# Down product of a hybrid decoder block: block results added to the residual in memory by one adding transfer

## The chip, the cores and the metric

The kernel runs on one core of one Trainium2 chip, in one launch. The metric is device time in microseconds. The engines are named as the profile names them: PE is TensorE (matmul), PEld its weight loads, DVE is VectorE, ACT is ScalarE, POOL is GpSimd, SP is SyncE, which here only issues transfers. The time before is 2142.49 us, the median of three runs (2139.59 to 2144.26).

## The reference

One decoder block on 512 rows of width 2048, in float32: a normalised input goes through a projection into two token mixers, their concatenated outputs through an output projection onto the residual, and then comes the channel mixer, which is where the change lies:

```python
x = x + jnp.einsum('bse,ed->bsd', y, w_out[l])
h = _rmsnorm(x, norm2_g[l])
up = jnp.einsum('bsd,df->bsf', h, ffn_w_up[l])          # 2048 -> 12288
up = _causal_dwconv(up, ffn_conv_w[l], ffn_conv_b[l])
gate, val = jnp.split(up, 2, axis=-1)
x = x + jnp.einsum('bsf,fd->bsd', jax.nn.gelu(gate) * val, ffn_w_down[l])  # 6144 -> 2048
return _rmsnorm(x, final_g)
```

## The kernel before, in words

**Matmul form.** A float32 operand is split into a rounded part h (ACT copy, L115) and the rest l (DVE subtraction, L116), and a product is three matmuls, h·h, h·l and l·h. The up and down products also use a fast scheme of seven block products for a 2 by 2 block product (the Strassen–Winograd form). A *unit* is one weight tile of four 128 by 256 pieces: it is loaded (512 KB, SP queue), VectorE forms three sums of its pieces (`sums`, L585 to L587; for activations L610 to L612), and the seven resulting operands are split (`pair`, L115 and L116). A unit is then 7 products of 6 matmuls (L753), 42 in all, issued in the order `ORDER = (1, 2, 6, 5, 3, 7, 4)`.

**PSUM.** Each of the seven products accumulates in a bank of its own over all units of a block; there are eight banks in rotation, so the next block's first product has a free bank, and each later one needs a bank that has been read out by ScalarE or VectorE.

**Stages.** The up product runs 24 blocks of 8 units; the seven results of a block are combined by `combine` (one ACT copy, seven VectorE operations) into two padded tiles, on which the width-3 convolution, the gelu and the gating work in later steps. The gated rows are stored to memory as `ad`. The down product has K = 6144 cut into three chunks of 8, 8 and 6 units and a tail of 512, and the output into four columns n of 512. It runs 12 blocks (chunk, column), each `size` units long. The residual of each column lives in memory as `x2d[n]`, 512 x 512 float32, 1 MB, laid out as 128 partitions of 8 KB. The tail does the last 512 of K with plain matmuls, one output row group at a time, together with the final norm.

**A down block.** In its second unit (in the seventh for the first block) GpSimd issues the load of `x2d[n]` into `xs[n]`, one of two 8 KB-per-partition tiles (L854, L855). At the block's end four ACT copies and three VectorE additions read the seven banks (L863 to L869): each of the three additions adds one bank to one quarter of `xs[n]`. Eight more VectorE operations (L871 to L878) are postponed by `later` to the next block's first four units, two after each. After the last two, GpSimd stores `xs[n]` back to `x2d[n]` (L891). The last chunk's columns 2 and 3 are not stored but stay in SBUF for the tail; columns 0 and 1 are loaded again for it (L900).

**Order.** In this part each engine executes its instructions in the order in which the code emits them. `prepare(ready(u))` is emitted before unit u's matmuls and keeps three steps going along one stream of weight and activation items: loads two items ahead, sums one ahead, splits up to the item before unit u+3's. The stream's tiles are triple-buffered (raw, h and l). Around each change of chunk the eight activation items of the next chunk are interleaved with the weight items, so there VectorE and ScalarE have up to two items a unit. GpSimd's queue in the down product holds only the residual loads and stores, and at the end four loads of the final gain (L905).

Of the kernel before, what the change touches and what calls it, by code (L numbers as in the profile page):

```python
# [8 lines left out]
F32 = mybir.dt.float32  # L9
# [3 lines left out]
ALU = mybir.AluOpType  # L13

P = 128
# [3 lines left out]
NS = S // P  # L19
# [48 lines left out]
def hybrid_block(ctx: ExitStack, tc: tile.TileContext, x, xT, w_in, w_out, w_up, w_dn, w_dl, wab, wsT, vec, bs, vgb, fg, out):  # L68
    nc = tc.nc
    const = ctx.enter_context(tc.tile_pool(name="const", bufs=1))  # L70
    def pool(name, side, bufs=1):
        return tc.alloc_tile_pool(name=name, bufs=bufs, side=side, reuse_waits="tile")
# [395 lines left out]
    for i in range(2):  # L468
        for st in range(NS):
            t = vv[i][:, st]  # L470
# [5 lines left out]
    for i in range(2):  # L476
        ps = project(w_in, B_U + i, xg, True)
# [161 lines left out]
    stream = []  # L639
# [117 lines left out]
    def later(step, f):  # L757
        lazy.setdefault(step, []).append(f)

    def t_tile(name, shape, bufs=1):  # L760
        return pools["t"].tile(shape, F32, name=name, tag=name, bufs=bufs)
# [1 line left out]
    def flat(q):  # L763
        return q.rearrange("p t n -> p (t n)")

    def combine(q, c1, c11, c12, c21, c22):

        tt = nc.vector.tensor_tensor
        nc.scalar.copy(c1, q[1])
        tt(c11, c1, q[2], ALU.add)  # L770
        v, w = t_tile("v", [P, 2, 256]), t_tile("w", [P, 2, 256])
        tt(v, q[6], c1, ALU.subtract)
        tt(w, q[5], v, ALU.add)
        tt(c12, w, q[3], ALU.add)
        tt(c22, w, q[7], ALU.add)
        tt(v, v, q[7], ALU.add)
        tt(c21, q[4], v, ALU.subtract)

    gates = {}

    def up_block(g, val, u0):
        q = {}
        for m in range(8):
            prepare(ready(u0 + m))
            for p in ORDER:
                product(q, p, act[m], stream[place[u0 + m]].hl, True, m == 0, m == 7)
            if m == 7 and u0 == 0:
                pads[:] = [t_tile(f"pad{n}", [P, 2, S + 2]) for n in range(2)]
                for t in pads:
                    nc.gpsimd.memset(t[:, :, 0:2], 0.0)  # L790
            for f in lazy.pop(u0 + m, ()):
                f()
        c1 = t_tile("c1", [P, 2, 256])
        lo, hi = slice(2, 258), slice(258, 514)
        combine(q, c1, pads[0][:, :, lo], pads[1][:, :, lo], pads[0][:, :, hi], pads[1][:, :, hi])
        if u0 == 0:
            pools["ps"].release()
            pools["tr"].release()
            pools["ps"] = psum("q1", 8)

        def tap(n, j, f):
            if val:
                dst = t_tile("cv", [P, 2, S])if j == 0 else cvs[n]
                cvs[n] = dst
            else:
                if j == 0:
                    gates[n] = t_tile("gate", [P, 2, S], 2)
                dst = gates[n]
            nc.scalar.activation(dst[:, j], pads[n][:, j, 2:2 + S], AF.Identity, bias=col(V_FB + f), scale=col(V_FW + 2 * 96 + f))

        def rest(n, j, f):
            dst = (cvs if val else gates)[n][:, j]
            for i in (1, 0):
                nc.vector.scalar_tensor_tensor(dst, pads[n][:, j, i:i + S], col(V_FW + i * 96 + f), dst, ALU.mult, ALU.add)
            if val:
                gate = gates[n][:, j]
                nc.vector.tensor_tensor(gate, gate, dst, ALU.mult)
                at = 0 if j else 2
                nc.gpsimd.dma_start(ad[2 * g + n][:, at:at + 2], gate.rearrange("p (a b) -> p a b", a=2))  # L819

        def gelu(n, j):
            t = gates[n][:, j]
            nc.scalar.activation(t, t, AF.Gelu_apprx_tanh)

        cvs = {}
        at = u0 + 8
        for i, (n, j) in enumerate(((1, 0), (1, 1), (0, 0), (0, 1))):
            f = 48 * val + 4 * g + 2 * n + j
            step = at + (0, 1, 3, 4)[i]
            later(step, lambda n=n, j=j, f=f: tap(n, j, f))  # L830
            later(step + 1, lambda n=n, j=j, f=f: rest(n, j, f))
            if not val:
                later(step + 2, lambda n=n, j=j: gelu(n, j))
# [9 lines left out]
    def down_block(ci, n, u0):  # L843
        tt = nc.vector.tensor_tensor
        size = len(CHUNKS[ci])
        q = {}
        for m in range(size):
            prepare(ready(u0 + m))
            if m == (6 if u0 == n_up else 1):
                if u0 == n_up:  # L850

                    pools["t"].release()
                    pools["x"] = pool("tx", "right")
                xs[n] = pools["x"].tile([P, NS, 512], F32, name="xs", tag="xs", bufs=2)  # L854
                nc.gpsimd.dma_start(xs[n], x2d[n])  # L855
            for p in ORDER:
                product(q, p, act[m], stream[place[u0 + m]].hl, False, m == 0, m == size - 1)
            for f in lazy.pop(u0 + m, ()):
                f()
        X = xs[n]  # L860
        X11, X12, X21, X22 = X[:, 0:2, 0:256], X[:, 0:2, 256:512], X[:, 2:4, 0:256], X[:, 2:4, 256:512]
        c1, c6, c5, c7 = (pools["x"].tile([P, 2, 256], F32, name="cc", tag="cc", bufs=4) for _ in range(4))
        nc.scalar.copy(c1, q[1])  # L863
        tt(X11, X11, q[2], ALU.add)
        nc.scalar.copy(c6, q[6])
        nc.scalar.copy(c5, q[5])
        tt(X12, X12, q[3], ALU.add)
        nc.scalar.copy(c7, q[7])
        tt(X21, X21, q[4], ALU.add)  # L869
        steps = [  # L870
            lambda: tt(X11, X11, c1, ALU.add),  # L871
            lambda: tt(c6, c6, c1, ALU.subtract),
            lambda: tt(c5, c5, c6, ALU.add),
            lambda: tt(X12, X12, c5, ALU.add),
            lambda: tt(c6, c6, c7, ALU.add),
            lambda: tt(X21, X21, c6, ALU.subtract),
            lambda: tt(c5, c5, c7, ALU.add),
            lambda: tt(X22, X22, c5, ALU.add),  # L878
        ]
        if u0 + size == len(units):  # L880
            prepare(len(stream) - 2)
            for f in steps:
                f()
            prepare(len(stream) - 1)
            return
        at = u0 + size
        for i in range(4):
            later(at + i, steps[2 * i])
            later(at + i, steps[2 * i + 1])
        if ci < 2 or n < 2:  # L890
            later(at + 3, lambda: nc.gpsimd.dma_start(x2d[n], X))  # L891

    for ci, s in enumerate(starts):
        for n in range(4):
# [12 lines left out]
    for st in range(NS):  # L907
# [4 lines left out]
        for n, (i, d, lo, hi) in enumerate(pieces):  # L912
# [5 lines left out]
                mm3(ps, a, w, f == 0, f == 3)  # L918
            t = xs[d][:, st, lo:hi]
            nc.vector.tensor_tensor(t, t, ps, ALU.add)  # L920
            sq = pools["x"].tile([P, 512], F32, name="sq", tag="cc", bufs=4)
            nc.scalar.activation(sq[:, 0:hi - lo], t, AF.Square, accum_out=ss3[:, st, n:n + 1])
            if last_rows and n < 3:
                nc.gpsimd.tensor_tensor(t, t, fgb[d][:, lo:hi], ALU.mult)
# [13 lines left out]
        for n in order:  # L938
# [7 lines left out]
                nc.scalar.mul(t, t, r)  # L946
            eng = nc.scalar if last_rows and n % 2 == 0 else nc.sync
            eng.dma_start(out[st * P:(st + 1) * P, d * 512 + lo:d * 512 + hi], t)
    for p in (pools["x"], pools["ps"], pools["a2"], pools["a1"], wq):
        p.release()  # L950


# [51 lines left out]
```

## Time and profile before

| | |
|---|---|
| median of three runs | 2142.49 us (2139.59 to 2144.26) |
| the profiled execution | 2140.87 us |
| its span, first to last instruction | 2139.2 us |
| mean granted TensorE clock | 0.982 |
| PE busy | 2065.3 us (97%) |
| DVE busy | 1806.6 us (84%) |
| ACT busy | 905.5 us (42%) |
| POOL busy | 59.6 us (3%) |
| loads `xs<-x2d` | 12 of 1 MB, median 5.7 us from issue to landing |
| stores `x2d<-xs` | 10 of 1 MB, median 4.7 us in the down product |

The page gives busy time by engine, then the span in 40 slices of 53.5 us with a digit for the busy tenths of each. The up product takes roughly slices 12 to 30, the down product 31 to 39, the tail is the last one. Matmul records overlap, so a busy PE is not PE at its peak, and a few matmul records can be missing. A row of the timeline or of the chain of waits begins with its start in us from the span's start and its duration; a bracket behind a row gives the idle time of the engine before it and what ended it. A row of a group gives count, busy time, mean and idle time before.

### The profile page before, as it was taken

Reading aid. Unit: us, or ns where it says so; the run is one execution under the profiler, and the core shown is the slowest. Engines: PE = TensorE matmul, PEld = TensorE weight load, DVE = VectorE, ACT = ScalarE, POOL = GpSimd, SP = SyncE. Lnnn points to the kernel's source line nnn. Section 1 sums busy time; section 2 is a strip of 40 time slices with the busy share of each in tenths; the row PEclk is TensorE's granted clock in tenths of the full one; section 3 lists DMA queues with packets and bytes.
Section 4 is the critical chain, followed back from the end, with each engine's and each line's share of the span. In section 5 each row is a group of like instructions: output and inputs, shape, how many; then the busy total and the mean of one; then the engine's idle time right before and its main releaser. Section 6 shows DMA issues by size and latency. Waiting matters only on the chain.

```text
span 2139.2 us, 34631 instructions
## 1 busy us (share of the span) xinstructions
PE 2065.3 (97%) x14552; PEld 1944.5 (91%) x14552; DVE 1806.6 (84%) x2341; ACT 905.5 (42%) x891; POOL 59.6 (3%) x118
## 2 busy tenths in 40 slices
PE   9999999999789999999999999999988998999998
PEld 7888888888679999999999999999978997998996
DVE  7588972744369999999999999999999999989986
ACT  5445322413244444444444444444444344444443
POOL 0000000100000000000000000000000000000001
PEclk9999999999889999999999999999989999999999
DMA  6222322533013333333333333333335454544563
GB/s 233 87 93 85 112 88 96 172 134 138 40 50 119 116 114 121 117 118 119 119 119 119 119 119 119 119 117 121 119 119 174 149 172 166 179 148 166 197 214 121
DMA packets 68605, 275.14 MB, mean 129 GB/s; under 512 B 8160, under 2 KB 8800, under 8 KB 58720
## 3 DMA queue, kind: packets, MB, share of 16 engines
q1 hardware_dynamic: 57888, 224.01, 32.4%
q0 software_dynamic: 9984, 48.24, 6.1%
q8 instruction: 114, 1.87, 0.4%
q10 hardware_dynamic: 576, 0.66, 0.1%
q14 instruction: 43, 0.35, 0.0%
HBM read 241.43 MB, written 31.46 MB: 128 GB/s over the span
## 4 chain that ended last, share of the span: by engine, by line
PE 47%; issue 39%; DVE 10%; DMA 2%; ACT 1%; POOL 1%; SPq 0%; POOLq 0%; DVEq 0%; ACTq 0%
PE qs L753 18%; PE ps L153 8%; PE ps L151 8%; PE ps L152 8%; DVE wl L116 3%; DVE al L116 2%; POOL ad L819 1%; PE tr L673 1%; DVE q L585 1%; DMA q<-w_dn 1%; PE qs L152 1%; PE qs L153 1%; PE qs L151 1%; DVE q L610 1%; DMA q<-ad 1%
## 5 line engine op out<-in xcount | busy, mean ns | idle before, releaser
L753 PE MATMUL qs<-ah,wh 128*128 128x256 f32 x2688 | 765.1, 285 | 4.9 <-ACT ah L115 2.4
L753 PE MATMUL qs<-ah,wl 128*128 128x256 f32 x2688 | 764.1, 284 | 5.7 <-DVE wl L116 5.7
L753 PE MATMUL qs<-al,wh 128*128 128x256 f32 x2688 | 764.1, 284 | 1.5 <-DVE al L116 1.5
L115 ACT CAST wh<-q 128x1792 fp32r<-128x1792 f32 (+1 forms) x282 | 476.8, 1691 | 669.5 <-PE qs L753 437.4
L116 DVE TENSOR_TENSOR wl<-q,wh 128x1792 fp32r<-128x1792 f32 (+1 forms) x282 | 567.7, 2013 | 24.9 <-ACT wh L115 24.8
L753 PEld LDWEIGHTS qs<-ah,wl 128*128 128x128 f32 x2688 | 519.5, 193 | 6.1 <-DVE wl L116 6.1
L753 PEld LDWEIGHTS qs<-ah,wh 128*128 128x128 f32 x2688 | 519.6, 193 | 5.8 <-ACT ah L115 2.6
L753 PEld LDWEIGHTS qs<-al,wh 128*128 128x128 f32 x2688 | 519.6, 193 | 1.8 <-DVE al L116 1.8
L753 PE MATMUL qs<-wl,ah 128*128 128x256 f32 x1232 | 355.1, 288 | 16.4 <-DVE wl L116 16.4
L753 PE MATMUL qs<-wh,ah 128*128 128x256 f32 x1232 | 354.3, 288 | 9.6 <-ACT cc L863 4.1
L753 PE MATMUL qs<-wh,al 128*128 128x256 f32 x1232 | 353.8, 287 | 4.8 <-DVE al L116 4.8
L753 PEld LDWEIGHTS qs<-wl,ah 128*128 128x128 f32 x1232 | 241.5, 196 | 18.8 <-DVE wl L116 18.7
L753 PEld LDWEIGHTS qs<-wh,ah 128*128 128x128 f32 x1232 | 241.8, 196 | 11.2 <-ACT cc L863 4.5
L753 PEld LDWEIGHTS qs<-wh,al 128*128 128x128 f32 x1232 | 241.6, 196 | 5.2 <-DVE al L116 5.2
L116 DVE TENSOR_TENSOR wl<-wraw,wh 128x1024 fp32r<-128x1024 f32 (+2 forms) x105 | 118.1, 1126 | 147.6 <-ACT wh L115 147.3
L115 ACT CAST wh<-wraw 128x1024 fp32r<-128x1024 f32 (+2 forms) x105 | 102.2, 974 | 275.6 <-PE ps L152 145.3
L585 DVE TENSOR_TENSOR q<-q 128x512 f32<-128x512 f32 x280 | 191.9, 685 | 15.5 <-DMA q<-w_dn 9.2
L151 PE MATMUL ps<-xgh,wh 128*128 128x512 f32 x384 | 152.4, 397 | 1.7 <-ACT wh L115 1.7
L152 PE MATMUL ps<-xgl,wh 128*128 128x512 f32 x384 | 152.1, 397 | 0.0
L153 PE MATMUL ps<-xgh,wl 128*128 128x512 f32 x384 | 150.5, 397 | 0.0
L586 DVE TENSOR_TENSOR q<-q 128x256 f32<-128x256 f32 x280 | 119.0, 425 | 9.7
L587 DVE TENSOR_TENSOR q<-q 128x256 f32<-128x256 f32 x280 | 119.0, 425 | 9.6
(241 smaller groups left out, 2303.9 us busy)
## 6 DMA issues: line engine op xcount, KB each, us to landing
q<-w_up SPq DMA_DIRECT2D x192, 512.0 KB, 3.5
q<-w_dn SPq DMA_DIRECT2D x88, 512.0 KB, 3.5
wraw<-w_in SPq DMA_DIRECT2D x28, 1024.0 KB, 4.9
wraw<-w_out SPq DMA_DIRECT2D x16, 1024.0 KB, 4.9
ad<-gate POOLq DMA_DIRECT2D x48, 256.0 KB, 2.3
q<-ad SPq DMA_DIRECT2D x24, 512.0 KB, 3.2
xs<-x2d POOLq DMA_DIRECT2D x12, 1024.0 KB, 5.7
x2d<-xs POOLq DMA_DIRECT2D x10, 1024.0 KB, 4.7
```

The lines of the kernel that those rows point to most:

```text
L115: nc.scalar.copy(h, src)
L116: nc.vector.tensor_tensor(l, src, h.bitcast(F32), ALU.subtract)
L151: nc.tensor.matmul(ps, lhsT=ah, rhs=bh, start=start, stop=False)
L152: nc.tensor.matmul(ps, lhsT=ah, rhs=bl, start=False, stop=False)
L153: nc.tensor.matmul(ps, lhsT=al, rhs=bh, start=False, stop=stop)
L585: nc.vector.tensor_tensor(q[:, 2:4], q[:, 5:7], q[:, 7:8].broadcast_to([P, 2, 256]), ALU.add)
L586: nc.vector.tensor_tensor(q[:, 1], q[:, 2], q[:, 6], ALU.add)
L587: nc.vector.tensor_tensor(q[:, 0], q[:, 1], q[:, 4], ALU.add)
L610: nc.vector.tensor_tensor(q[:, 2:4], q[:, 7:8].broadcast_to([P, 2, 256]), q[:, 5:7], ALU.subtract)
L673: nc.tensor.matmul(ps[:, st * P:(st + 1) * P], lhsT=x2[k // 4][:, st, (k % 4) * P:(k % 4 + 1) * P], rhs=diag[st], start=True, stop=True)
L753: nc.tensor.matmul(q[p][:, t], lhsT=x_, rhs=y_, start=first and t == 0 and n == 0, stop=last and t == 1 and n == 2, skip_group_check=True)
L819: nc.gpsimd.dma_start(ad[2 * g + n][:, at:at + 2], gate.rearrange("p (a b) -> p a b", a=2))
```

## The change

In the down product, the block's result is no longer added to the residual by VectorE. `combine`, the routine of the up product, writes the four quarters of the result into a tile `c` of its own (two buffers of the size that the `xs` tiles had), and GpSimd issues one transfer from `c` to `x2d[n]` with `accum_op=ALU.add`, which adds the tile to what is in memory. This holds for the first eleven blocks. So the residual is not loaded for them, the eleven VectorE operations of a block become seven, all at the block's end and none postponed, and the four ACT copies become one. The last block (chunk 2, column 3) works as before; in its second unit the residuals of columns 2 and 3 are loaded, since column 2's now also goes through memory.

`combine` no longer gets a tile for its ACT copy: the copy goes into `v`, which the following operations overwrite in place. `v` and `w` are taken in turn from three buffers in the up product (four in the down product) in place of one tile each for the copy, `v` and `w`. The pool for the down product keeps the name `pools["t"]`.

```diff
-    def combine(q, c1, c11, c12, c21, c22):
+    def combine(q, c11, c12, c21, c22):
 
         tt = nc.vector.tensor_tensor
-        nc.scalar.copy(c1, q[1])
-        tt(c11, c1, q[2], ALU.add)
-        v, w = t_tile("v", [P, 2, 256]), t_tile("w", [P, 2, 256])
-        tt(v, q[6], c1, ALU.subtract)
+        v, w = (t_tile("cc", [P, 2, 256], 3 if pads_on[0] else 4) for _ in range(2))
+        nc.scalar.copy(v, q[1])
+        tt(c11, v, q[2], ALU.add)
+        tt(v, q[6], v, ALU.subtract)
         tt(w, q[5], v, ALU.add)
         tt(c12, w, q[3], ALU.add)
         tt(c22, w, q[7], ALU.add)
         tt(v, v, q[7], ALU.add)
         tt(c21, q[4], v, ALU.subtract)
...
             prepare(ready(u0 + m))
-            if m == (6 if u0 == n_up else 1):
-                if u0 == n_up:
-
-                    pools["t"].release()
-                    pools["x"] = pool("tx", "right")
-                xs[n] = pools["x"].tile([P, NS, 512], F32, name="xs", tag="xs", bufs=2)
-                nc.gpsimd.dma_start(xs[n], x2d[n])
+            if m == 6 and u0 == n_up:
+
+                pools["t"].release()
+                pools["t"] = pool("tx", "right")
+                pads_on[0] = False
+            if m == 1 and u0 + size == len(units):
+                for d in (2, 3):
+                    xs[d] = t_tile("cx", [P, NS, 512], 2)
+                    nc.gpsimd.dma_start(xs[d], x2d[d])
             for p in ORDER:
                 product(q, p, act[m], stream[place[u0 + m]].hl, False, m == 0, m == size - 1)
             for f in lazy.pop(u0 + m, ()):
                 f()
+        lo, hi = slice(0, 256), slice(256, 512)
+        if u0 + size < len(units):
+            c = t_tile("cx", [P, NS, 512], 2)
+            combine(q, c[:, 0:2, lo], c[:, 0:2, hi], c[:, 2:4, lo], c[:, 2:4, hi])
+            nc.gpsimd.dma_start(x2d[n], c, accum_op=ALU.add)
+            return
+
         X = xs[n]
...
-        at = u0 + size
-        for i in range(4):
-            later(at + i, steps[2 * i])
-            later(at + i, steps[2 * i + 1])
-        if ci < 2 or n < 2:
-            later(at + 3, lambda: nc.gpsimd.dma_start(x2d[n], X))
```

More of the change, by code (lines that the diff above doesn't have):

```diff
@@ L777, in combine @@
         tt(c21, q[4], v, ALU.subtract)
+    pads_on = [True]
     gates = {}
@@ L792, in up_block @@
                 f()
-        c1 = t_tile("c1", [P, 2, 256])
         lo, hi = slice(2, 258), slice(258, 514)
-        combine(q, c1, pads[0][:, :, lo], pads[1][:, :, lo], pads[0][:, :, hi], pads[1][:, :, hi])
+        combine(q, pads[0][:, :, lo], pads[1][:, :, lo], pads[0][:, :, hi], pads[1][:, :, hi])
         if u0 == 0:
@@ L859, in down_block @@
                 f()
+        lo, hi = slice(0, 256), slice(256, 512)
[4 more added lines that the diff above has]
+            return
         X = xs[n]
-        X11, X12, X21, X22 = X[:, 0:2, 0:256], X[:, 0:2, 256:512], X[:, 2:4, 0:256], X[:, 2:4, 256:512]
-        c1, c6, c5, c7 = (pools["x"].tile([P, 2, 256], F32, name="cc", tag="cc", bufs=4) for _ in range(4))
+        X11, X12, X21, X22 = X[:, 0:2, lo], X[:, 0:2, hi], X[:, 2:4, lo], X[:, 2:4, hi]
+        c1, c6, c5, c7 = (t_tile("cc", [P, 2, 256], 4) for _ in range(4))
         nc.scalar.copy(c1, q[1])
@@ L869, in down_block @@
         tt(X21, X21, q[4], ALU.add)
[L870 to L885, printed above, removed]
-        at = u0 + size
-        for i in range(4):
-            later(at + i, steps[2 * i])
-            later(at + i, steps[2 * i + 1])
-        if ci < 2 or n < 2:
-            later(at + 3, lambda: nc.gpsimd.dma_start(x2d[n], X))
+        prepare(len(stream) - 2)
+        tt(X11, X11, c1, ALU.add)
+        tt(c6, c6, c1, ALU.subtract)
+        tt(c5, c5, c6, ALU.add)
+        tt(X12, X12, c5, ALU.add)
+        tt(c6, c6, c7, ALU.add)
+        tt(X21, X21, c6, ALU.subtract)
+        tt(c5, c5, c7, ALU.add)
+        tt(X22, X22, c5, ALU.add)
+        prepare(len(stream) - 1)
     for ci, s in enumerate(starts):
@@ L920, in hybrid_block @@
             nc.vector.tensor_tensor(t, t, ps, ALU.add)
-            sq = pools["x"].tile([P, 512], F32, name="sq", tag="cc", bufs=4)
+            sq = t_tile("cc", [P, 512], 4)
             nc.scalar.activation(sq[:, 0:hi - lo], t, AF.Square, accum_out=ss3[:, st, n:n + 1])
@@ L948, in hybrid_block @@
             eng.dma_start(out[st * P:(st + 1) * P, d * 512 + lo:d * 512 + hi], t)
-    for p in (pools["x"], pools["ps"], pools["a2"], pools["a1"], wq):
+    for p in (pools["t"], pools["ps"], pools["a2"], pools["a1"], wq):
         p.release()
```

## The prediction, made before the changed kernel was run

> **What bounds the kernel now.** I read the page's span and 40 slices first, then the windows by stage, the chain of waits, and VectorE's timeline along the chain. Blocks are named chunk.column, so 0.2 is chunk 0, column 2.
>
> ```profile
> span 2139.2 us, 34631 instructions
> DVE  7588972744369999999999999999999999989986
> 1655.90:1733.20 77.30, 77.30 (x644) 77.30 (x645) 69.19 (x87) 29.82 (x23) 2.13 (x4) 1.00 0.49 171
> 1733.20:1834.20 101.00, 89.07 (x702) 87.20 (x700) 95.01 (x118) 46.14 (x33) 2.13 (x4) 0.97 0.50 167
> 1834.20:1911.60 77.40, 77.36 (x644) 77.36 (x645) 69.34 (x88) 29.79 (x23) 2.13 (x4) 1.00 0.51 165
> 1911.60:1987.80 76.20, 68.19 (x548) 67.13 (x546) 72.69 (x91) 34.13 (x23) 1.06 (x2) 0.98 0.46 152
> 1987.80:2083.70 95.90, 95.90 (x787) 95.89 (x788) 89.35 (x111) 42.55 (x38) 3.20 (x6) 0.98 0.62 210
> ```
>
> In the digit row VectorE is at nine tenths or more from slice 13 on, nearly to the end. The windows (stretch, length, then TensorE, its weight loads, VectorE, ScalarE, GpSimd busy with counts, granted clock, DMA share, GB/s) split the down product in two kinds of stretch. In the first, third and fifth TensorE never stops: 644 matmuls in 77.3 us, 0.120 us each. In the second and fourth it does: 702 matmuls would need 84.3 us and took 101.0, 548 would need 65.8 and took 76.2. So 16.7 + 10.4 = 27 us is the most that anything done for VectorE can return there. The chain of waits (start, us, what) has the same borders, a DVE row where TensorE stops setting the time and a PE row where it starts again:
>
> ```profile
> 1655.87 77.31 PE qs L753 x642
> 1733.20 0.69 DVE xs L869
> ...
> 1834.24 77.32 PE qs L753 x642
> 1911.58 0.69 DVE xs L869
> ```
>
> Between 1733.2 and 1834.2 (stretch A) and between 1911.6 and 1987.8 (stretch B) the chain consists of VectorE's instructions and of loads that VectorE waits for. These are the stretches in which the next chunk's activations are split beside the weights. A VectorE operation taken away there shortens the kernel; in the other stretches it lies beside TensorE.
>
> **VectorE's work per block.** Its timeline (start, us, line) at the end of block 0.3, at the first and last pair of postponed steps of block 0.2, and at a combine of the up product:
>
> ```profile
> 1782.94 0.68 DVE L864 TENSOR_TENSOR xs<-xs,qs 128x512 f32<-128x512 f32 x1
> ...
> 1784.73 0.68 DVE L610 TENSOR_TENSOR q<-q 128x512 f32<-128x512 f32 x1
> 1737.27 0.69 DVE L871 TENSOR_TENSOR xs<-xs,cc 128x512 f32<-128x512 f32 x1
> ...
> 1738.47 0.69 DVE L610 TENSOR_TENSOR q<-q 128x512 f32<-128x512 f32 x1
> 1758.44 0.68 DVE L877 TENSOR_TENSOR cc<-cc 128x512 f32<-128x512 f32 x1
> ...
> 1759.77 0.68 DVE L610 TENSOR_TENSOR q<-q 128x512 f32<-128x512 f32 x1
> 1463.73 0.68 DVE L770 TENSOR_TENSOR pad<-c,qs 128x512 f32<-128x512 f32 x1
> ...
> 1468.51 0.68 DVE L585 TENSOR_TENSOR q<-q 128x512 f32<-128x512 f32 x1
> ```
>
> Before: L864, L867 and L869 take 1784.73 − 1782.94 = 1.8 us. The eight postponed steps are four pairs; the first takes 1.20 us (1737.27 to 1738.47) and I give the other three the 1.33 us of the last (1758.44 to 1759.77), 5.2 together. That is 7.0 us for eleven operations. After: seven operations in the same order and on the same operand kinds as the up product's combine, which takes 1468.51 − 1463.73 = 4.8 us, more than seven times 0.6, because some read the result just written. Saved per block: **2.2 us**, not four elevenths. Of the eleven blocks that change, the cut lies on the chain for 0.2 and 0.3 (stretch A) and 1.2 and 1.3 (stretch B): 4 × 2.2 = **8.8 us**. For the other seven I take nothing, their cover being TensorE, whose windows have no gap; without that cover they would give up to 15 us more.
>
> The seven operations now come in one piece, so VectorE gets to the next weights 4.8 − 1.8 = 3.0 us later. TensorE has two split units ahead at that point (the schedule splits unit u+2 before unit u), 84 matmuls or 10 us. Combine 4.8, sums 1.5 and a split of 2.0 make 8.3 us; this fits. The bank order is also kept: the banks of products 6, 5 and 7 were freed by ScalarE copies and are now freed by VectorE in ORDER, about 0.7 us apart, against the 0.72 us that TensorE needs for a product (6 × 0.120). Three ScalarE copies a block go; ScalarE is under half busy in every window, so nothing for them. In the up product the number of operations is the same: nothing.
>
> **Transfers.** VectorE's waits for transfers on the chain (waited time in brackets), the lengths from issue to landing, and when the residual's loads were issued:
>
> ```profile
> 1655.12 0.69 DVE L864 TENSOR_TENSOR xs<-xs,qs 128x512 f32<-128x512 f32 x1 [0.67 <-DMA xs<-x2d]
> 1772.40 0.69 DVE L610 TENSOR_TENSOR q<-q 128x512 f32<-128x512 f32 x1 [2.11 <-DMA q<-ad]
> 1826.59 0.69 DVE L585 TENSOR_TENSOR q<-q 128x512 f32<-128x512 f32 x1 [1.82 <-DMA q<-w_dn]
> 1946.12 0.69 DVE L585 TENSOR_TENSOR q<-q 128x512 f32<-128x512 f32 x1 [0.97 <-DMA q<-w_dn]
> 1950.75 0.69 DVE L610 TENSOR_TENSOR q<-q 128x512 f32<-128x512 f32 x1 [1.08 <-DMA q<-ad]
> q<-w_dn SPq DMA_DIRECT2D x79, 512.0 KB, 3.5
> xs<-x2d POOLq DMA_DIRECT2D x12, 1024.0 KB, 5.7
> x2d<-xs POOLq DMA_DIRECT2D x10, 1024.0 KB, 4.7
> 1765.00 0.53 POOL L855 DMA_DIRECT2D xs<-x2d  x1 [4.32 <-DMA x2d<-xs]
> 1819.15 0.53 POOL L855 DMA_DIRECT2D xs<-x2d  x1 [4.12 <-DMA x2d<-xs]
> 1943.77 0.53 POOL L855 DMA_DIRECT2D xs<-x2d  x1 [4.70 <-DMA x2d<-xs]
> ```
>
> The first row is block 0.0 waiting for its residual; it releases TensorE at 1655.87. That load goes: **0.7 us** gained. The other four waits are 2.11 + 1.82 + 0.97 + 1.08 = 6.0 us, and each follows a residual load by some 2 to 8 us, itself issued as soon as the store before it had landed. Three such pairs of store and load cost 6.0 us, 2.0 a pair. The reason stands in the rows: one weight item on VectorE is sums 1.5 + split 2.0 = 3.5 us, and a weight load lands in 3.5 us, so whatever makes a load later is waited for in full when VectorE is the bound. All these pairs go.
>
> Instead each block issues one adding transfer of 1 MB, right after its combine, four of them in or at the head of stretches A and B. No trace of before shows one. From below: it hides whole, 0. A plain store's 4.7 us, half a pair, would cost 1.0. From above by the longest that the rows give: a pair one after the other, 4.7 + 5.7 = 10.4 us, long enough to run beside three loads of 3.5 us at 2.0 each, 6. It reads the block, reads memory and writes memory, three of a pair's four passes, and no postponed step now stands between two weight items to cover a late load. I take a little over a pair, **2.3 us** each, 9.2 in all: 9.2 − 6.0 = 3.2 us more than now. GpSimd pays one issue instead of two, and waits there hold up nothing but later residual transfers.
>
> *A rule weighed against this.* The Trainium skill, "Collectives: The Full Stack", Part 3 on the bandwidth ceiling, says that a transfer that adds is slow because it reads two sources through one ring, not because of the addition; for ring collectives it gives half the rate. By it the estimate for 1 MB is twice the store, 9.4 us, and the sum becomes that of the second rival below, 2144.
>
> **The end.** The last block keeps its residual in SBUF, and now also fetches column 2:
>
> ```profile
> 2057.50 0.68 DVE L864 TENSOR_TENSOR xs<-xs,qs 128x512 f32<-128x512 f32 x1
> 2081.68 0.68 DVE L864 TENSOR_TENSOR xs<-xs,qs 128x512 f32<-128x512 f32 x1
> 2083.72 0.69 DVE L867 TENSOR_TENSOR xs<-xs,qs 128x512 f32<-128x512 f32 x1 [1.35 <-PE qs L753]
> 2070.78 7.74 SPq L629 DMA_DIRECT2D q<-w_dl  x3
> ```
>
> Block 2.2's combine starts at 2057.5, ends 4.8 us later, and the adding transfer is out at about 2062.8. Column 2's load must wait for it on GpSimd's queue, and column 3's load stands behind that one. With 7 us for the adding transfer (between 4.7 and 10.4) the loads go at 2070 and 2070.5, beside three 1 MB weight loads in the 7.7 us from 2070.78; at 5.7 us each, one behind the other, they land by about 2081.5. L864 needs column 3 at 2081.7 and has 1.35 us to spare before L867's wait for TensorE. So anything over 8 us for the adding transfer is paid at the end one for one. Bounds: 0 to 5 us lost (10.4 instead of 7, plus the weight loads' share); I take **1 us**. The final column's loads behind them wait for TensorE now, and still will.
>
> **Sum.** 0.7 + 8.8 − 3.2 − 1 = 5.3 us gained. The profiled execution took 2140.87 us (its span is 2139.2, 1.7 us lie around it), so 2135.6. That execution is 1.6 us below the median of the runs, 2142.49; on that scale 2137.
>
> **Rivals.**
> 1. *The adding transfer is as cheap as a store.* 1.0 us each, nothing at the end: 0.7 + 8.8 + 6.0 − 4.0 = 11.5 gained, 2131. For it: one transfer replaces two, and no load waits for a store any more. With no wait at all, 15.5 gained, 2127. Against: the lost cover.
> 2. *No change: it reaches two loads instead of one.* 4 us each, 16 in all, 10 more than now, and 1 us at the end: 0.7 + 8.8 − 10 − 1 = 1.5 lost, 2144. For it: a weight item and a weight load are both 3.5 us, so there is no slack for a transfer of 9 us. Against: pairs of that length cost 2.0 now. (The rule above would make it this one; no run so far shows whether it holds.)
> 3. *Slower: the engines that add also carry the weights.* If an adding transfer goes at a fraction of a copy's rate, packets of weights queue behind its packets in stretches A and B. It decides from 3.9 us of waiting each (15.5 over four). At 6 us each, the upper bound, and 5 us at the end: 24 − 15.5 + 5 = 13.5 lost, 2156. For it: the last block would have its residual late as well. Against: DMA is busy about half the time in A and B.
> That VectorE's cut is hidden anyway would also be no change; the chain of waits speaks clearly against it, and I count it under the second.
>
> **Chances.** Forecast 0.38 (4 to 9 us gained, 2133 to 2139), first rival 0.18, second 0.22, third 0.22. A difference under 0.2% (4.3 us) can't be told from none here. The forecast gives 0.34 to faster and 0.04 to same, the first rival all to faster, the second 0.20 to same and 0.02 to slower, the third all to slower: 0.52, 0.24, 0.24. The range goes from 2126, all waits gone, to 2152, which leaves out the worse half of the third rival.
>
> **What would show it.** VectorE: seven operations of 4.8 us at each block's end, no postponed steps; stretches A and B about 4 us shorter each before transfers are counted; no residual load before the last block. Right on transfers, if waits of "q" loads behind each adding transfer are near 2 us and its landing near 7. Wrong, if it lands after more than 10, if waits per block exceed 4, or if L864 of the last block waits for xs. If VectorE waits for TensorE within A or B, the chain was misread.

## The result, and the profile after

| | before | after |
|---|---|---|
| median of five runs each, side by side | 2141.87 us (2139.22 to 2144.26) | 2152.56 us (2149.89 to 2153.48) |
| ratio | | 1.0050, 95% interval 1.0035 to 1.0064 |
| span of the profiled execution | 2139.2 us | 2150.9 us |
| mean granted clock | 0.982 | 0.980 |

The kernel became 10.7 us slower; the forecast was 5 us faster. The page of the changed kernel (span; VectorE's total and digit row; the adding transfers with their size and the median time from issue to landing):

```profile
span 2150.9 us, 34620 instructions
DVE  7588972744369999999999999999999889889976
...
x2d<-cx POOLq DMA_DIRECT2D x11, 1024.0 KB, 7.8
```

VectorE did get lighter: some of the nines after slice 31 have become eights, and its busy time fell from 1806.6 to 1784.5 us, 22.1 us, which is eleven blocks by 2.0. The time went up all the same. To see where, I counted the matmul records from the last handover of the up product (336 a block, 252 in the last chunk) and compared when the last one of each block starts. The column "before" is the time from that handover, the others are the difference to it. The experiments' columns are explained below.

| end of block | before | after | e1 | e2 | e3 | e6 | e7 | e13 |
|---|---|---|---|---|---|---|---|---|
| 0.0 | 51.7 | +1.6 | +1.4 | +1.4 | +0.1 | 0.0 | +0.2 | +0.4 |
| 0.1 | 92.6 | +2.9 | +1.7 | +2.8 | +3.1 | −0.6 | −0.4 | −0.1 |
| 0.2 | 132.9 | +2.9 | +1.7 | +2.8 | +3.1 | −0.6 | −0.4 | −0.1 |
| 1.0 | 229.6 | +4.3 | +5.0 | −0.5 | +5.2 | +2.9 | −2.7 | −3.9 |
| 1.2 | 311.3 | +5.5 | +4.0 | +0.6 | +9.0 | +1.9 | −3.7 | −4.9 |
| 2.0 | 394.1 | +4.6 | +4.3 | −3.1 | +9.7 | +4.0 | −3.1 | −5.6 |
| 2.1 | 424.3 | +6.7 | +4.3 | −1.7 | +12.2 | +4.0 | −3.1 | −5.6 |
| 2.2 | 454.6 | +6.7 | +4.3 | −1.7 | +12.2 | +4.0 | −3.1 | −5.6 |
| 2.3 | 484.9 | +10.2 | +5.6 | +1.8 | +14.3 | +8.1 | −2.8 | −5.6 |

After: 1.6 us are lost in block 0.0; 1.3, 1.2 and 2.1 at the handovers 0.0 to 0.1, 1.0 to 1.1 and 2.0 to 2.1; 1.4 and −0.9 in the two stretches where VectorE sets the time (0.2's end to 1.0's, 1.2's to 2.0's), where the forecast had a gain of 5.6; and 3.5 in the last block. Together 10.2 us. The tail is the same. The spans differ by 11.7 us; 2.0 of these lie ahead of the first handover, where executions scatter: e3, which has the instructions of before up to there, reaches it 2.7 us later than before.

**The handovers.** TensorE's timeline at the first one (start, us, what; in the bracket how long it had stood and for whom), after:

```profile
1657.50 0.39 PE L753 MATMUL qs<-wh,ah 128*128 128x256 f32 x1 [0.48 <-DVE cx L771]
1659.43 0.39 PE L753 MATMUL qs<-wh,ah 128*128 128x256 f32 x1 [0.16 <-DVE cc L773]
1661.51 0.36 PE L753 MATMUL qs<-wh,ah 128*128 128x256 f32 x1 [0.31 <-DVE cc L776]
```

and before:

```profile
1655.87 0.38 PE L753 MATMUL qs<-wh,ah 128*128 128x256 f32 x1 [0.31 <-DVE xs L864]
```

By the count of records these are matmuls 12, 24 and 36 of block 0.1 after, and matmul 30 before. TensorE used to have free banks for five products of the next block when VectorE began; now it has two, and then follows the chain of `combine` and stops at every second product. ScalarE's timeline shows who used to free them. Before:

```profile
1650.82 0.58 ACT L863 COPY cc<-qs 128x512 f32<-128x512 f32 x1
1651.30 0.59 ACT L865 COPY cc<-qs 128x512 f32<-128x512 f32 x1
1651.77 0.60 ACT L866 COPY cc<-qs 128x512 f32<-128x512 f32 x1
1652.25 0.61 ACT L868 COPY cc<-qs 128x512 f32<-128x512 f32 x1
```

After, there is one of them, and VectorE's first operation comes 3.5 us later, behind a split:

```profile
1653.21 0.58 ACT L770 COPY cc<-qs 128x512 f32<-128x512 f32 x1
```

```profile
1656.76 0.68 DVE L771 TENSOR_TENSOR cx<-cc,qs 128x512 f32<-128x512 f32 x1
...
1658.69 0.69 DVE L773 TENSOR_TENSOR cc<-qs,cc 128x512 f32<-128x512 f32 x1 [0.46 <-DVE cc L772]
...
1660.68 0.68 DVE L776 TENSOR_TENSOR cc<-cc,qs 128x512 f32<-128x512 f32 x1
```

From L771's end at 1657.44 to L776's at 1661.36 VectorE frees five banks, 0.98 us apart on average; TensorE needs 0.72 us for a product.

The waits, summed over the down product from 1640 us on (who waits for whom: us in total, times, longest), have it once more. After, then before:

```profile
DVE q L585 <- DMA q<-w_dn: 30.8, 18, 3.6
PE qs L753 <- DVE cx L771: 10.0, 6, 2.7
```

```profile
DVE q L585 <- DMA q<-w_dn: 9.2, 7, 1.9
PE qs L753 <- DVE xs L864: 1.3, 3, 0.7
```

**The transfers.** The other pair of rows is VectorE waiting for weights: 30.8 us against 9.2. VectorE's timeline in the first of its stretches, from the first combine to the fourth wait:

```profile
1736.77 0.68 DVE L771 TENSOR_TENSOR cx<-cc,qs 128x512 f32<-128x512 f32 x1
...
1741.74 0.68 DVE L585 TENSOR_TENSOR q<-q 128x512 f32<-128x512 f32 x1
...
1752.31 0.69 DVE L585 TENSOR_TENSOR q<-q 128x512 f32<-128x512 f32 x1 [3.58 <-DMA q<-w_dn]
...
1763.88 0.69 DVE L585 TENSOR_TENSOR q<-q 128x512 f32<-128x512 f32 x1 [1.12 <-DMA q<-w_dn]
...
1802.73 0.69 DVE L585 TENSOR_TENSOR q<-q 128x512 f32<-128x512 f32 x1 [2.29 <-DMA q<-w_dn]
```

The seven operations take 4.97 us. Behind each adding transfer stands a wait; the second transfer of this stretch goes out at 1793.83. With one of 0.24 us they are 7.2 us in this stretch, and in the other 5.1 us (2.15, 0.19, 2.28, 0.17 and 0.27): 12.3 us. The DMA queues say what an adding transfer costs the 16 DMA engines. In the 12 us around block 0.2's transfer after, and in 16 us of before that hold one residual load and one store (packets, MB, share of the 16 engines' time):

```profile
q0 software_dynamic: 144, 1.05, 47.3%
```

```profile
q0 software_dynamic: 288, 2.10, 34.1%
```

47.3% of 12 us is 5.7 us of all engines for one adding transfer; 34.1% of 16 us is 5.5 us for the load and the store together. So the adding transfer is a pair's work, but in one piece and just when VectorE goes back to the weights.

**The last block.** TensorE (first row), then GpSimd, VectorE:

```profile
2066.78 0.38 PE L753 MATMUL qs<-wh,ah 128*128 128x256 f32 x1 [1.79 <-DVE cx L771]
```

```profile
2080.73 1.10 POOL L857 DMA_DIRECT2D cx<-x2d  x2 [8.47 <-issue]
```

```profile
2083.29 0.69 DVE L585 TENSOR_TENSOR q<-q 128x512 f32<-128x512 f32 x1 [2.28 <-DMA q<-w_dn]
...
2093.77 0.69 DVE L873 TENSOR_TENSOR cx<-cx,qs 128x512 f32<-128x512 f32 x1 [1.37 <-PE qs L753]
```

L873 is the old L864. It doesn't wait for the residual: columns 2 and 3 are there in time. All of the 3.5 us arise in the block's first unit, 8.6 us for 42 matmuls against 5.1 before: the bank stop of 1.79 us, and slower matmuls for some 4 us behind it. The other five units take 5.0 us each, as before, so VectorE's wait of 2.28 us for weights beside the two residual loads held up nothing on TensorE.

### The profile page after: what moved, and what is told of

It is laid out like the page before. It is cut to its first block, busy times and chain, and to the rows that moved or that the text cites. A ratio compares the mean times of both kernels' runs of the same rounds, so it can differ in the third digit from the quotient of the medians.

```text
span 2150.9 us, 34620 instructions
## 1 busy us (share of the span) xinstructions
PE 2071.0 (96%) x14552; PEld 1948.7 (91%) x14552; DVE 1784.5 (83%) x2297; ACT 888.2 (41%) x858; POOL 58.5 (3%) x109
## 5 line engine op out<-in xcount | busy, mean ns | idle before, releaser
L115 ACT CAST wh<-q 128x1792 fp32r<-128x1792 f32 (+1 forms) x282 | 476.6, 1690 | 688.6 <-PE qs L753 421.8
L585 DVE TENSOR_TENSOR q<-q 128x512 f32<-128x512 f32 x280 | 191.8, 685 | 37.6 <-DMA q<-w_dn 30.8
L115 ACT CAST wh<-wraw 128x1024 fp32r<-128x1024 f32 (+2 forms) x105 | 102.2, 974 | 275.6 <-PE ps L152 145.3
```

The costliest lines, as they stand in the source:

```text
L115: nc.scalar.copy(h, src)
L585: nc.vector.tensor_tensor(q[:, 2:4], q[:, 5:7], q[:, 7:8].broadcast_to([P, 2, 256]), ALU.add)
```

## The experiments

The kernel before was timed beside each experiment. Its medians lie between 2141.5 and 2143.2 us, so ratios to it are given. Their intervals reach 2 to 3 us to either side, so a difference of that size between two experiments says little.

### Banks: ScalarE reads them again (e1)

```diff
-            combine(q, c[:, 0:2, lo], c[:, 0:2, hi], c[:, 2:4, lo], c[:, 2:4, hi])
...
+            for t, p in ((c1, 1), (c6, 6), (c5, 5), (c7, 7)):
+                nc.scalar.copy(t, q[p])
+            tt(c11, c1, q[2], ALU.add)
+            tt(c6, c6, c1, ALU.subtract)
+            tt(c5, c5, c6, ALU.add)
+            tt(c12, c5, q[3], ALU.add)
...
```

> The changed kernel, with one thing put back: products 1, 6, 5 and 7 are read out of their banks by four ScalarE copies, as in the kernel before, and VectorE combines from the copies; the adding transfer stays. Theory 1 (banks): the 11 us were lost because TensorE must wait for VectorE's combine to get its banks, in the four places where it overtakes VectorE (ends of blocks 0.0, 1.0, 2.0, 2.2), some 3 us each. Then 9 to 11 us come back: 2142 to 2144 us, and no wait of TensorE for the last steps of the combine. Theory 2 (transfers): the 11 us are weight loads held up by the adding transfers. Then nothing comes back: 2151 to 2154 us.

Measured: 2149.04 us, ratio 1.0031 (1.0019 to 1.0042). That is 3.5 us back of the 10.7, less than expected. TensorE's first handover shows both halves:

```profile
1662.96 0.39 PE L753 MATMUL qs<-wh,ah 128*128 128x256 f32 x1 [0.19 <-DVE cx L872]
```

One stop instead of three, now at matmul 36 and for the fourth VectorE operation, which alone reads product 3's bank. The handover 2.0 to 2.1 costs nothing any more (+4.3 to +4.3, where after lost 2.1), the first 0.3 instead of 1.3. But the stretch from the end of 0.2 to the end of 1.0 now loses 3.3 us where after lost 1.4, which takes part of it back.

### The addition left out (e2, e4)

```diff
-            nc.gpsimd.dma_start(x2d[n], c, accum_op=ALU.add)
+            nc.gpsimd.dma_start(x2d[n], c)
```

In e2 this is done to the changed kernel, in e4 to e1.

> The changed kernel with a plain store of the block's result in place of the adding transfer (the addition to the residual is left out, 1 MB goes out and nothing is read). Theory 1 (banks): VectorE's waits for loads in the two stretches that it bounds fall from 12.3 us to about 4, so 5 to 8 us come back, 2145 to 2148 us, and the waits of TensorE at block ends stay. Theory 2 (transfers): all of it comes back and the saved VectorE work too, 2138 to 2142 us.

> Both of the above on the changed kernel: four ScalarE copies, and a plain store instead of the adding transfer (the addition to the residual is left out). Theory 1 with transfers as a smaller second cause: the two gains add up, 15 to 18 us below the changed kernel, 2134 to 2138 us. Theory 2: as with the plain store alone, within 2 us of it.

Measured: e2 2144.97 us, 1.0010 (1.0001 to 1.0019); e4 2141.72 us, 0.9995 (0.9986 to 1.0004). So the price of adding, with the same bytes to send, is 7.6 us in the changed kernel and 7.3 in e1; the copies are worth 3.3 us here and 3.5 there, little more than the uncertainty. As far as it allows to say, the two causes add up. By the table e2 ends 8.4 us ahead of after, of which 7.6 come between the ends of 0.2 and 2.0, where the two VectorE stretches lie. With both undone e4 is level with before, although VectorE does the lighter work. In its profile the last block alone loses 5.8 us, 4.5 of them in the last unit, to one wait of VectorE of 7.3 us for weights.

### The mechanism alone, in the kernel before (e3)

The three ScalarE copies that free the banks of products 6, 5 and 7 are held back until VectorE's first addition is done, by a one-column copy that reads its result. Transfers and VectorE's work stay as they were.

```diff
         tt(X11, X11, q[2], ALU.add)
+        nc.scalar.copy(c6[:, 0, 0:1], X11[:, 0, 0:1])
         nc.scalar.copy(c6, q[6])
```

> The kernel before, with ScalarE's copies of products 6, 5 and 7 held until VectorE has done its first addition of the block (a ScalarE copy of one column that reads what VectorE wrote stands ahead of them); transfers and VectorE's work are as before. Theory 1 (banks): TensorE stops after two or three products of the next block, not five, wherever VectorE is late: 2 us in each of four places, 2148 to 2152 us. Theory 2 (transfers): no difference, 2140 to 2144 us.

Measured: 2155.78 us, ratio 1.0060 (1.0046 to 1.0073), 13.0 us slower. TensorE's timeline shows the stops, at matmul 12 of blocks 0.1, 1.1 and 2.1:

```profile
1657.99 0.39 PE L753 MATMUL qs<-wh,ah 128*128 128x256 f32 x1 [1.83 <-DVE xs L864]
...
1842.28 0.39 PE L753 MATMUL qs<-wh,ah 128*128 128x256 f32 x1 [2.48 <-DVE xs L864]
...
2010.39 0.39 PE L753 MATMUL qs<-wh,ah 128*128 128x256 f32 x1 [2.22 <-DVE xs L864]
```

In the table the column steps at the same places as after: +3.0 at 0.1, +2.5 by 2.1. The three stops are 6.5 us together. ScalarE, which stands at the added copy, also makes the split behind it later (its L115 begins 57.0 us from the last handover of the up product, in the kernel before 52.8), so not all of the 13.0 us need be banks. But who frees the banks, and when, is enough by itself to stop TensorE and make this kernel slower, without any change in bytes or in VectorE's work. It isn't the size of the effect in the changed kernel: e3 holds back copies that the changed kernel doesn't have.

### Column 2 kept in SBUF (e9)

The changed kernel, but in the last chunk column 2 is treated as in the kernel before: its residual is loaded in its own second unit and stays in SBUF.

```diff
-            if m == 1 and u0 + size == len(units):
-                for d in (2, 3):
-                    xs[d] = t_tile("cx", [P, NS, 512], 2)
-                    nc.gpsimd.dma_start(xs[d], x2d[d])
+            if m == 1 and ci == 2 and n > 1:
+                xs[n] = t_tile("cx", [P, NS, 512], 2)
+                nc.gpsimd.dma_start(xs[n], x2d[n])
...
-        if u0 + size < len(units):
+        if ci < 2 or n < 2:
...
```

> The changed kernel, with column 2 of the last chunk as in the kernel before (residual loaded, result kept in SBUF, four ScalarE copies, postponed additions); the ten other blocks as in the changed kernel. It prices the last block by itself. Theory 1: 2.5 to 4 us come back, 2148 to 2150 us, since a wait of TensorE at the end of block 2.2 and the doubled residual loads go. Theory 2: about 1 us, one adding transfer of eleven.

Measured: 2153.70 us, ratio 1.0048 (1.0035 to 1.0060), the same as after. In its one profile the last block is some 2 us shorter than after's, but the median doesn't show it. What the last block loses, 1.8 us here and 3.5 in after, it loses in its first unit, ahead of the residual loads of after at 2080.73. That column 2 now goes through memory isn't what made the kernel slower.

### All seven banks copied, the sums postponed (e6, e8)

ScalarE copies all seven products, three of them straight into `c`; the seven VectorE operations then work on SBUF alone and are postponed, two a unit; the transfer of 1 MB goes out after the last. Column 2 as in e9. e8 is e6 with a plain store, the addition left out.

```diff
...
+            for t, p in ((c1, 1), (c11, 2), (c6, 6), (c5, 5), (c12, 3), (c7, 7), (c21, 4)):
+                nc.scalar.copy(t, q[p])
+            at = u0 + size
+            later(at, lambda: tt(c6, c6, c1, ALU.subtract))
+            later(at, lambda: tt(c11, c11, c1, ALU.add))
...
+            later(at + 3, lambda: tt(c21, c21, c6, ALU.subtract))
+            later(at + 3, lambda: nc.gpsimd.dma_start(x2d[n], c, accum_op=ALU.add))
```

> All seven products are read out of their banks by ScalarE copies (three of them straight into the tile that is added to memory), VectorE's seven operations work on SBUF alone and are postponed, two after each unit of the next block, and the adding transfer follows the last of them. Column 2 of the last chunk stays in SBUF with the residual loaded, as in the kernel before, so the last block fetches one residual. Theory 1 (banks, with transfers and the last block's loads as smaller causes): no wait of TensorE for VectorE at a block's end, none of the 3.5 us lost in the last block; the saved VectorE work (8.8 us) less the adding transfers' longer waits (6 us) remains: 2137 to 2142 us, level with the kernel before or some us faster. Theory 2 (the adding transfers alone cost the 11 us): 2150 us and more.

> As e6_seven_copies, with a plain store in place of the adding transfer (the addition to the residual is left out for ten of the twelve blocks). It prices the addition by itself where banks hold nothing up. Theory 1: 6 to 9 us faster than e6_seven_copies, 2130 to 2134 us. Theory 2: 10 us and more faster.

Measured: e6 2150.79 us, 1.0038 (1.0026 to 1.0051); e8 2135.21 us, 0.9962 (0.9950 to 0.9975). The handovers into 0.1, 1.1 and 2.1 are clean now (e6 stands at −0.6 at the end of 0.1 and of 0.2), yet the adding transfer takes all of it back and more: 15.6 us between e6 and e8. The three longest of VectorE's waits in e6, each over within 11 us of an adding transfer's issue (1760.98, 1814.58 and 1941.80):

```profile
1771.62 0.69 DVE L585 TENSOR_TENSOR q<-q 128x512 f32<-128x512 f32 x1 [4.01 <-DMA q<-w_dn]
1825.01 0.69 DVE L585 TENSOR_TENSOR q<-q 128x512 f32<-128x512 f32 x1 [3.81 <-DMA q<-w_dn]
```

```profile
1952.66 0.69 DVE L585 TENSOR_TENSOR q<-q 128x512 f32<-128x512 f32 x1 [4.24 <-DMA q<-w_dn]
```

e8 shows what the design would be worth if adding were free: 7.9 us.

### Adding, or bytes (e12)

e6 with two plain stores of 1 MB, one behind the other, in place of the adding transfer; the addition is left out.

```diff
-            later(at + 3, lambda: nc.gpsimd.dma_start(x2d[n], c, accum_op=ALU.add))
+            later(at + 3, lambda: nc.gpsimd.dma_start(x2d[n], c))
+            later(at + 3, lambda: nc.gpsimd.dma_start(x2s[n], c))
```

> As e6_seven_copies, but two plain stores of 1 MB, one behind the other, to two places in memory, in place of one adding transfer (the addition to the residual is left out for ten of the twelve blocks). By the profile an adding transfer takes about 5.7 us of all 16 engines per MB and a plain one 2.7, so the two stores take about as much. If the time on the engines is all that the addition costs: as e6_seven_copies, 2148 to 2152 us. If an adding transfer holds each weight packet longer than plain ones do: between the one store and the adding transfer, 2137 to 2143 us.

Measured: 2152.19 us, ratio 1.0042 (1.0028 to 1.0055), no different from e6. In 18 us around block 0.2's pair the engines spent 30.1% of their time on it:

```profile
q0 software_dynamic: 288, 2.10, 30.1%
```

and in the same 18 us of e6 on the one adding transfer 33.1%:

```profile
q0 software_dynamic: 144, 1.05, 33.1%
```

5.4 and 6.0 us. There is nothing special in adding: it keeps the DMA engines busy for as long as two copies of its size, and two copies in the same place delay the weights as much.

### In pieces (e7, e10, e11, e13)

If what counts is how much is in flight at once beside the weight loads, smaller transfers further apart should be cheaper. e7 sends e6's block in two halves, the upper when its quarters are done, the lower at the end:

```diff
+            later(at + 1, lambda: nc.gpsimd.dma_start(x2d[n][:, 0:2], c[:, 0:2], accum_op=ALU.add))
...
-            later(at + 3, lambda: nc.gpsimd.dma_start(x2d[n], c, accum_op=ALU.add))
+            later(at + 3, lambda: nc.gpsimd.dma_start(x2d[n][:, 2:4], c[:, 2:4], accum_op=ALU.add))
```

> As e6_seven_copies, but the result goes out in two adding transfers of 512 KB, the first after the second pair of VectorE's operations, the second at the end. If a weight load is held up by the length of what is in flight, a half holds it up by half, and part of it lies under the postponed operations: 2 to 4 us faster than e6_seven_copies. If the engines' time for adding is what counts, the same within 1 us.

Measured: 2141.55 us, ratio 0.9993 (0.9984 to 1.0002): 9.2 us better than e6, level with before. The waits where e6 had 4.01 and 3.81:

```profile
1770.39 0.69 DVE L585 TENSOR_TENSOR q<-q 128x512 f32<-128x512 f32 x1 [1.23 <-DMA q<-w_dn]
...
1822.07 0.69 DVE L585 TENSOR_TENSOR q<-q 128x512 f32<-128x512 f32 x1 [1.53 <-DMA q<-w_dn]
```

Then quarters: e10 cuts e7's halves into row groups of 256 KB (shown), e11 does that to the changed kernel's transfer.

```diff
+            for i in range(4):
+                later(at + 1 + i, lambda i=i: nc.gpsimd.dma_start(x2d[n][:, i:i + 1], c[:, i:i + 1], accum_op=ALU.add))
```

> As e7_two_halves, but the result goes out in four adding transfers of 256 KB, one after each of four units of the next block. If the length of what is in flight beside a weight load decides (theory 1, second part), a quarter costs a load about 1.4 us, which the postponed VectorE operations cover: 2 to 4 us faster than e7_two_halves, 2137 to 2140 us, faster than the kernel before. If the sum of the engines' time decides, as e7_two_halves within 1 us.

> The changed kernel with nothing altered but the transfer: four adding transfers of 256 KB, one after each of the next block's first four units (for column 2 of the last chunk all four at once). VectorE's operations and the banks are as in the changed kernel. If banks and transfers are separate causes: 6 to 9 us come back, 2143 to 2147 us, and TensorE's waits for the combine at block ends stay. If the transfers alone were the cause: 2139 to 2142 us. If their length does not matter: 2151 to 2154 us.

Measured: e10 2141.50 us, 0.9994 (0.9985 to 1.0002), as e7; e11 2153.14 us, 1.0051 (1.0038 to 1.0063), as after. But neither tested what it was meant to. GpSimd's timeline (e11, then e10; x2 is two issues in one row):

```profile
1740.52 1.75 POOL L867 DMA_DIRECT2D x2d<-cx  x2 [36.59 <-DVE cx L774]
1742.51 1.75 POOL L867 DMA_DIRECT2D x2d<-cx  x2 [0.24 <-DVE cx L777]
```

```profile
1749.98 1.75 POOL L877 DMA_DIRECT2D x2d<-cx  x2 [32.73 <-DVE cx L872]
1762.17 1.75 POOL L877 DMA_DIRECT2D x2d<-cx  x2 [10.44 <-DVE cx L875]
```

I had handed the issues out over four units in the code. That spaces nothing: GpSimd has no other work and issues each as soon as its rows are ready, so e11's four left within 4 us and e10's in two pairs, as e7's halves.

e13 ties each piece to the operation that finishes it, so the data spaces them. A piece is now a quarter of the block as `combine` makes it: two row groups by 256 columns, in runs of 1 KB.

```diff
+            def send(rows, cols):
+                nc.gpsimd.dma_start(x2d[n][:, rows, cols], c[:, rows, cols], accum_op=ALU.add)
...
+            later(at, lambda: tt(c11, c11, c1, ALU.add))
+            later(at, lambda: send(top, lo))
+            later(at, lambda: tt(c6, c6, c1, ALU.subtract))
+            later(at + 1, lambda: tt(c5, c5, c6, ALU.add))
+            later(at + 1, lambda: tt(c12, c12, c5, ALU.add))
+            later(at + 1, lambda: send(top, hi))
+            later(at + 2, lambda: tt(c22, c5, c7, ALU.add))
+            later(at + 2, lambda: send(low, hi))
...
```

> The kernel of e7_two_halves with its two adding transfers of 512 KB replaced by four of 256 KB, each issued after the VectorE operation that finishes its quarter, so that they leave in four different units of the next block. If what is in flight at once decides: 2136 to 2139, 2 to 5 us faster than e7_two_halves, and faster than the kernel before. If pieces of 512 KB are already small enough, or if the shorter rows of 1 KB and two more issues cost what the spacing gives: 2140 to 2143, as e7_two_halves. If shorter rows cost the engines clearly more: over 2144.

Measured: 2135.73 us (2135.14 to 2137.40) against 2141.52, ratio 0.9970 (0.9959 to 0.9982). It is 5.8 us faster than the kernel before, with the same computation, and close to e8, which doesn't add at all (0.9962). GpSimd's timeline in the first VectorE stretch:

```profile
1740.86 1.19 POOL L869 DMA_DIRECT2D x2d<-cx  x1 [24.45 <-DVE cx L873]
1750.59 1.21 POOL L869 DMA_DIRECT2D x2d<-cx  x1 [8.54 <-DVE q L586]
1753.76 1.19 POOL L869 DMA_DIRECT2D x2d<-cx  x1 [1.97 <-DVE cx L879]
1761.87 1.20 POOL L869 DMA_DIRECT2D x2d<-cx  x1 [6.92 <-DVE cx L882]
```

Four issues over 21 us. The waits of the whole down product (30.8 us after, 27.2 in e6), and the landing of a piece:

```profile
DVE q L585 <- DMA q<-w_dn: 6.0, 8, 1.7
```

```profile
x2d<-cx POOLq DMA_DIRECT2D x40, 256.0 KB, 4.9
```

In the table e13 gains in the two VectorE stretches and loses nothing at the handovers or in the last block: that is the forecast's picture, in a kernel that does two things more.

## Why the prediction was wrong, point by point

Forecast −5.3 us, the profile +10.2, so 15.5 us to account for. By place: block 0.0, −0.7 forecast and +1.6 measured, 2.3; the three handovers into 0.1, 1.1 and 2.1, nothing forecast and 4.6 measured; the two VectorE stretches with the handovers at their ends, −5.6 forecast and +0.5 measured, 6.1; the last block, +1 forecast and +3.5 measured, 2.5.

**The step that failed: "The bank order is also kept … about 0.7 us apart, against the 0.72 us that TensorE needs for a product", costed at nothing.** The order was kept. The spacing was not 0.7 us but 0.98 on average, since some operations wait for the one before (0.46 us at L773) and the bank of product 7 is read twice; this gives the stops at matmuls 24 and 36. And the spacing isn't all: what decides the first stop is when the first bank comes free. ScalarE had read four banks by 1652.9, about a microsecond after the block's last matmul (51.7 us from the handover at 1599.97); VectorE is a split behind at that point. TensorE's head start fell from five products to two, and it then waits for the first operation of the burst and on along the chain. The sentence on the copies that go, "ScalarE is under half busy in every window, so nothing for them", was the same mistake from the other side: they were not there for load but to free banks early.

By place, this step accounts for most of the 15.5: the 2.3 and the 4.6 (block 0.0's loss belongs to the first handover, as shown below), the 2.5 of the last block, and 1.4 at the ends of the VectorE stretches. e3 shows the mechanism in the kernel before. Putting four copies back gives 3.3 to 3.5 us (e1 and e4 against after and e2), since TensorE then still stops at the seventh product. With seven (e6, e7, e13) no handover into 0.1, 1.1 or 2.1 loses anything, and where the store is plain the step from one copy to seven is worth 10.3 us (e2 1.0010, e8 0.9962; e8 also postpones the seven operations and treats column 2 as in e9).

**The term that was mis-sized: "2.3 us each, 9.2 in all".** Measured 12.3 us of waits in the two stretches, 3.1 each, against the 6.0 of before: 3.1 us more than forecast. The first waits behind three of the four transfers, 2.15 to 2.29, are near the forecast; the excess is mostly behind block 0.2's, 3.58 and then 1.12. The reasoning was right, that a late load is waited for in full where VectorE is the bound; "a little over a pair" was right for the work of the DMA engines, 5.7 us against 5.5 for a load and a store. What I missed is that a pair comes in two pieces with postponed work between. e7 and e13 show that spacing is what the price hangs on: 9.2 us back by halves, and nearly all of it by spaced quarters. Of the rest of the 6.1, 1.4 us are TensorE's bank stops at the ends of the stretches (VectorE, from L771 to L771 against L864 to L864, takes 0.9 us less in the two stretches together, TensorE 0.5 more), and 1.6 lie on VectorE, part of it the saving of 2.0 us a block for 2.2, the rest idle time that I didn't trace.

**The rule on a transfer with two sources** (the Trainium skill, "Collectives: The Full Stack", Part 3 on the bandwidth ceiling) holds here for the engines: 5.7 us of engine time per MB against 2.6 for a plain store (21.6% of 12 us in e2), a factor of about two. The runs show the factor, not its reason. The landing that I estimated from it, 9.4 us, was 7.8 as the median of the eleven and 9.4 for block 0.2's. The waits of 4 us each that go with it in the second rival are e6's (4.01, 3.81, 4.24), not after's 3.1.

**The third rival** had the right sign and one of the causes. By its own condition, 3.9 us of waits each, it wasn't reached in the changed kernel: 12.3 us are less than the 15.5 that VectorE and the old waits were to give back. That doesn't clear the transfers. With the banks freed early the kernel is still slower than before (e1 by 6.3 us; e6, whose longest waits are about 4 us, by 7.6), and only without the addition (e4, e8) or with the transfer spaced (e7, e10, e13) is it level or faster. Of the 7.6 us that adding costs over a plain store in the changed kernel, the forecast had 5.2 in its sum (2.3 against 1.0 for each of four), so most of this price was foreseen.

**What held.** Seven operations in 4.97 us against 4.8 forecast, 2.0 us saved a block against 2.2. The borders of the stretches. "This fits", on the units split ahead: at 1661.51 TensorE goes on without a stop for splits, so the burst is covered in that respect. In the last block, that L873 wouldn't wait for the residual, and that the final loads stay covered; the 1 us taken for them was not paid, and the 3.5 us lost there are the bank stop of 1.79 us and the slow matmuls behind it.

**Block 0.0's 1.6 us** arise in its last unit, 11.3 us for 42 matmuls against 10.0, at a reduced granted clock (below). By themselves they are no cost of the change: e11 has the same instructions as after up to this point and took 9.8 us; e7 and e10 also share theirs and took 10.0 and 11.1. In the changed kernel the stop behind the unit gives back what a slow unit takes, since VectorE's burst comes no later. e11 stops here for 1.82 us where after has 0.48, and at the end of block 0.1 the two stand at +3.2 and +2.9:

```profile
1657.51 0.38 PE L753 MATMUL qs<-wh,ah 128*128 128x256 f32 x1 [1.82 <-DVE cx L771]
```

**What stays open.** It wasn't tested why the adding transfer costs 7.6 us in the changed kernel and 15.6 in e6, beyond that e6's waits behind it are longer, and that 4.1 us of its loss lie in the last block, where an addition of VectorE that frees a bank comes late behind a wait for weights of 2.66 us and TensorE stops for 2.39. And with neither cause left e8 gains 7.9 us, not the 11.5 that the first rival's sum gave for a transfer as cheap as a store; where the rest went wasn't traced.

## What to carry to other kernels

Before moving work off an engine that looks idle, ask what it frees and when: a copy that empties a bank early is worth the head start it gives the next block, whatever its own time. A bulk transfer beside a just-in-time stream of loads should be priced by how much of it is in flight at once; cut it into pieces and let each hang on the operation that produces it, because giving the issues to later steps of the code spaces nothing on a queue that has no other work. Where an optimisation moves work from one place to several, look at each part separately: here the idea was worth 5.8 us, and how it was placed cost 17 (2152.56 against 2135.73).

## What the runs showed of the hardware

An adding transfer of 1 MB takes 5.7 to 6.0 us of all 16 DMA engines, two plain stores of 1 MB 5.4 us, one 2.5 to 2.6; it lands in 7.8 us (median in the changed kernel; 9.5 in e6) against 4.7 to 5.3. In pieces of 256 KB with runs of 1 KB it costs more, not less: 26.8% of 8 us for one piece,

```profile
q0 software_dynamic: 272, 0.26, 26.8%
```

2.1 us, or 8.6 us per MB, and the kernel with these pieces is still the fastest that adds. So the engines' total time wasn't the bound here, the place of it was.

The granted clock is lower in the windows behind a stall of TensorE of a few microseconds. Those of 5 us at the end of block 0.0, where TensorE had stood 3.07 us for a split, before and after (stretch, length, busy us of the engines with counts, granted clock, DMA share, GB/s):

```profile
1645.00:1650.00 5.00, 4.58 (x25) 4.58 (x26) 4.86 (x8) 1.05 (x2) 1.61 (x3) 0.66 0.55 166
1650.00:1655.00 5.00, 5.00 (x44) 5.00 (x43) 4.38 (x5) 4.46 (x6) 0.00 (x0) 1.00 0.95 349
```

```profile
1650.00:1655.00 5.00, 5.00 (x29) 5.00 (x29) 4.86 (x8) 2.17 (x2) 0.54 (x1) 0.60 0.39 129
```

At 0.60, 29 matmuls ran in 5 us, at 1.00 44. Where such a window lies, a stop costs more than its own length, but for how long differs between executions, as the last unit of block 0.0 in after and e11 shows (11.3 and 9.8 us). The Trainium skill, "TensorE: Matmul & The Clock Gate", Part 1, says that the clock falls to half after an idle window of about 3.4 us. The rows agree as far as they go: a stop of that size is followed by slow matmuls, and 0.60 is a mean over a window that holds both rates. But in after's last block a stop of 1.79 us was followed by slow matmuls too (a granted clock of 0.68 from 2066.66 to 2072), and one of 1.69 us at 1777.92 was not (1.00 from 1777.90 to 1784.00), which that figure doesn't give.
